# The end of the attention stage in a two-layer decoder trunk: when stored head outputs are read back, where one pair's output is kept, and which engine adds it up

## The chip, the core and the metric

One core of one Trainium2 chip runs the whole program in one launch. The metric is the device time of one execution in microseconds (us). The engines are TensorE (PE in the profile), VectorE (DVE), ScalarE (ACT), GpSimd (POOL) and SyncE (SP), which in this kernel issues nearly all DMAs.

## What is computed

A sequence of 1024 rows of width 1024 passes through two layers. Layer 0 is a recurrent mixer (RG-LRU) and a SwiGLU feed-forward network, layer 1 is stick-breaking attention with 16 heads of 64 columns and a second feed-forward network. Cut to the part that the change touches:

```python
def stick_breaking_attention(x, w_qkv, w_o):
    qkv = jnp.einsum("bsd,de->bse", x, w_qkv).reshape(bsz, seq, 3, N_HEADS, HEAD_DIM)
    ...
    for blk in range(seq // Q_BLOCK):
        z = jnp.einsum("bhqd,bhkd->bhqk", qb, kb).astype(jnp.float32) * scale
        strict = s_idx < t_idx
        log_fail = jnp.where(strict, jax.nn.log_sigmoid(-z), 0.0)
        suffix = lax.cumsum(log_fail, axis=3, reverse=True) - log_fail
        weights = jnp.where(strict, jnp.exp(jax.nn.log_sigmoid(z) + suffix), 0.0)
        outs.append(jnp.einsum("bhqk,bhkd->bhqd", weights.astype(vb.dtype), vb))
    o = jnp.concatenate(outs, axis=2)
    o = jnp.transpose(o, (0, 2, 1, 3)).reshape(bsz, seq, N_HEADS * HEAD_DIM)
    return jnp.einsum("bse,ed->bsd", o, w_o)
```

All is float32. The kernel splits each float32 operand of a dense product into a high and a low part and multiplies three times (`mm3`: high by high, high by low, low by high; lines 143, 144 and 145).

## The kernel before

**Pairs and halves.** The 16 heads are worked as 8 pairs, q = 0 to 7, and the sequence as two halves, n (or G) = 0 and 1, of 512 columns. The normalized input of the attention stands in SBUF as `xh[k][n]` and `xl[k][n]`, the high and low parts of row block k (128 rows of the model's width) and half n. The profile shows these buffers under the names of the tiles that had the space last: vh and vl, or xg. For each pair `qkv_steps` multiplies all eight row blocks with the pair's query, key and value weights (which = 0, 1, 2), 16 `mm3` each. The last reader of `xh` and `xl` is the value product of the last pair, (q, which) = (7, 2): first its eight row blocks for n = 0, then for n = 1.

**The loop.** The order of the work is written out by hand. A loop over u runs from -10 to 191; each u has one unit of `av_part` (a block of weights times values), one chunk of scores, two steps of the `qkv_steps` generator while it lasts, and a turn of small queued tasks. A chunk goes: PE makes scores (`z_part`, L1680 and L1681), ACT takes a sigmoid out of PSUM (`z_rest`, L1693), DVE scans it (`scan`, L1700 and L1703), ACT and DVE cut it into two 16-bit parts (`turn_weights`, L1713 and L1714, tile wx with four buffers), and SP issues a transposing DMA (L1717 to tile wd, L1721 to tile wt); other blocks are turned by PE itself (L1732) and cut by ACT (L1741) and DVE (L1742). PE then multiplies with the values (L1760). `last_two` is 168, the first unit of the last pair.

**Queued tasks.** `stage(task, steps)` holds a task for that many turns; `due()` runs what is due at the start of each u. `later` holds tasks of which each u runs one. The list `back` holds DMAs that read stored outputs back; each u issues one of them on SP (L1883), and from u = 160 on each even u two.

**Outputs.** A pair's output half (q, G) is gathered from PSUM by ACT (L1772) and DVE (L1773) into the tile oo, `add_v` adds a value term (tile vt) to it (L1777: GpSimd for the pairs 0 to 5, DVE for 6 and 7), and `parts` cuts it into a high part on ACT (L1784) and a low part on DVE (L1785). The output belongs into `xh[q]` and `xl[q]`, in which the normalized input still stands. So, for pairs that `kept(q, n)` names (0 to 5, and 6 for n = 0), `store` writes both parts to DRAM (tiles odh and odl, L1794 and L1795), and `bring_back` queues the reading back: for each half, once the last pair's value product of that half has been taken out of PSUM (L1610 to L1612).

**The values.** `evacuate` takes the value product out of PSUM (L1608), forms differences (L1613), and two turns later ACT makes a 16-bit copy (`high`, L1628), a turn later DVE its low part (L1618), and SP issues two transposing DMAs (L1622).

**What comes after.** From u = 163 on `out_fill` runs the first products of the output projection beside the last pair (tile ob, `mm3` with `xh[k][n]` for k = 0 to 6): one `mm3` in each of u = 163 to 168 for k = 0 to 5 of half 0, then k = 6 and the seven of half 1 in u = 177 to 180, then seven more from u = 182 on. The rest of the projection (tile ob_ps) and the second feed-forward network follow.

Of the kernel before, what the change touches and what calls it, by code (L numbers as in the profile page):

```python
# [34 lines left out]
def trunk(  # L35
# [21 lines left out]
    nc = tc.nc  # L57
# [84 lines left out]
    def mm3(ps, wh, wl, mh, ml, first, last, **kw):  # L142
        nc.tensor.matmul(ps, lhsT=wh, rhs=mh, start=first, stop=False, **kw)  # L143
        nc.tensor.matmul(ps, lhsT=wh, rhs=ml, start=False, stop=False, **kw)  # L144
        nc.tensor.matmul(ps, lhsT=wl, rhs=mh, start=False, stop=last, **kw)  # L145
# [1326 lines left out]
    NP = HEADS // 2  # L1472
# [3 lines left out]

    UP = 2.0**15

    kept = lambda q, n: q < NP - 2 + (n == 0)
    od = {  # L1480
        (q, n): [dp.tile([P, NB], F32, name=f"od{x}{q}_{n}") for x in "hl"]
        for n in range(NH)
# [5 lines left out]
    with ExitStack() as st:  # L1488
# [31 lines left out]
        def stage(task, steps=1):  # L1520
            soon.append([steps, task])
# [49 lines left out]
        def qkv_steps(q):  # L1571
            for which in range(3):
                w, at = wq.pop((q, which)), 3 * q + which + 1
                if at < 3 * NP:
                    raw = raws.pop(at)
                    wq[divmod(at, 3)] = next_weights(raw)
                    if which == 1:
                        later.extend(column_norms(raw, q))
                else:
                    mix[0].w[mix[0].order[0]] = next_weights(mix[0].raw.pop(0))  # L1580
                for i in (at + 1,) if at < 3 * NP else (at + 1, at + 2):
                    load_link(i)

                ks = (1, 5, 2, 6, 3, 7, 0, 4) if (q, which) == (0, 0) else range(ND)
                for n in range(NH):
                    pool, tag = (psZ, "z") if (q, which) == (0, 0) else (psQ, "qk")
                    ps = pool.tile([P, NB], F32, tag=tag, name="qk_ps")
                    for i, k in enumerate(ks):
                        mm3(ps, w[0][:, k], w[1][:, k], xh[k][n], xl[k][n], i == 0, i == ND - 1)
                        if i < ND - 1:  # L1590
                            yield
                    ev = evacuate(q, which, n, ps)
                    next(ev)
                    yield
                    next(ev, None)


        def evacuate(q, which, n, ps):
            full = lambda tag, m: [ap.tile([P, m, S], F32R, tag=tag, name=tag, bufs=4 if m == 1 else 3) for _ in range(2)]
            cs = slice(n * NB, (n + 1) * NB)  # L1600
            if which == 2:
                if n == 0:
                    VT[q] = ap.tile([P, S + 1], F32, tag="vt", name="vt", bufs=2)
                    nc.gpsimd.memset(VT[q][:, 0:1], 0.0)
                    VV[q] = ap.tile([P, 2, NT, 2, HD], F16, tag="v", name="v", bufs=2)
                t = ap.tile([P, NB], F32, tag="t", name="t", bufs=1)
                after = VT[q][:, n * NB + 1 : (n + 1) * NB + 1]
                nc.vector.scalar_tensor_tensor(after, ps, f32(sv[q]), rbc[n], op0=ALU.mult, op1=ALU.mult)  # L1608
                yield
                if q == NP - 1:  # L1610
                    some = [(p, n) for p in range(NP - 2)]
                    bring_back(*some[:3], *([(NP - 2, 0)] * n), *some[3:])  # L1612
                nc.vector.tensor_sub(t, VT[q][:, cs], after)  # L1613
                vx = ap.tile([P, 4, 2, P], F16, tag="vx", name="vx", bufs=2)
                t3 = t.rearrange("p (b c) -> p b c", b=4)

                def low():
                    nc.vector.scalar_tensor_tensor(  # L1618
                        vx[:, :, 1], t3, 1 / UP, vx[:, :, 0], op0=ALU.mult, op1=ALU.subtract
                    )  # L1620
                    for hx, a in enumerate((top, bot)):
                        nc.sync.dma_start(  # L1622
                            VV[q][:, hx, 4 * n : 4 * n + 4].rearrange("p b h c -> p (b h) c"),
                            vx[a].rearrange("p b h c -> p (b h c)"),
                            transpose=True,
                        )
                def high():
                    nc.scalar.activation(vx[:, :, 0], t3, AF.Copy, scale=1 / UP)  # L1628
                    stage(low)

                stage(high, 2)
                return
            two = ap.tile([P, 2, NB], F32R, tag="two", name="two", bufs=2)

            def spread():
                for hx, (a, b) in enumerate(((top, bot), (bot, top))):
                    if which == 0:
                        nc.sync.dma_start(f32(Q[q][hx])[a, cs], f32(two)[a, 0])
                        nc.sync.dma_start(f32(Q[q][hx])[b, cs], f32(two)[a, 1])
                    else:  # L1640
                        for half_ in (top, bot):
                            nc.sync.dma_start(f32(KK[q][hx])[half_, :, cs], f32(two)[a])

            def low():
                nc.vector.tensor_sub(two[:, 1], t, f32(two)[:, 0])
                stage(spread)

            if which == 0:
                t = ps
                if n == 0:  # L1650
                    Q[q] = [x[:, 0] for x in full("q", 1)]
                nc.scalar.copy(two[:, 0], t)
                yield
                low()
            else:
                t = f32(two)[:, 1]
                nc.vector.tensor_mul(t, ps, rbc[n])
                if n == 0:
                    KK[q] = full("kk", 2)
                yield  # L1660

                def high():
                    nc.scalar.copy(two[:, 0], t)
                    stage(low)

                stage(high)
# [80 lines left out]
        def av_part(tht, q, hx, G, kb, first, last):  # L1747
            q0 = (max(kb, 4 * G) - 4 * G) * P
            if first:
                av[0] = psO.tile([P, NB], F32, tag="o", name="av_ps")  # L1750
            ps = av[0]
            if kb // 4 != G:
                turned = [T[q, hx][:, 2 * kb + x].rearrange("p j c -> p (j c)") for x in range(2)]
                parts_ = [(0, NB, t, 0) for t in turned]
            else:
                parts_ = [(NB - P, NB, T[q, hx, 4 * G + 3][:, 2 * (kb % 4) + x], 0) for x in range(2)]
                if tht is not None:
                    parts_ = [(q0, NB - P, t, q0) for t in tht] + parts_
            for i, (c0, c1, t, t0) in enumerate(parts_):
                nc.tensor.matmul(  # L1760
                    ps[:, c0:c1], lhsT=VV[q][:, hx, kb], rhs=t[:, t0 : t0 + c1 - c0],
                    start=first and i == 0, stop=last and i == len(parts_) - 1,
                )
            if not last:
                return
            a, b = (top, bot)[:: 1 if hx == 0 else -1]

            def gather():
                if hx == 0:
                    oo[q, G] = ap.tile([P, NB], F32, tag="oo", name="oo", bufs=2)  # L1770
                o = oo[q, G]
                nc.scalar.copy(o[a], ps[b])  # L1772
                nc.vector.tensor_add(o[a], ps[a], o[a])  # L1773

            def add_v():
                eng = nc.vector if q >= NP - 2 else nc.gpsimd
                eng.tensor_add(oo[q, G], oo[q, G], VT[q][:, G * NB + 1 : (G + 1) * NB + 1])  # L1777

            def parts():
                o = oo[q, G]  # L1780
                down = f32(av_[q])

                def both(hi, lo):
                    nc.scalar.activation(hi, o, AF.Copy, scale=down)  # L1784
                    nc.vector.scalar_tensor_tensor(lo, o, down, f32(hi), op0=ALU.mult, op1=ALU.subtract)  # L1785

                if not kept(q, G):
                    both(xh[q][G], xl[q][G])
                else:
                    oh = ap.tile([P, NB], F32R, tag="oh", name="oh", bufs=1)  # L1790
                    both(oh, o.bitcast(F32R))

                    def store():
                        nc.sync.dma_start(od[q, G][0], f32(oh))  # L1794
                        nc.sync.dma_start(od[q, G][1], o)  # L1795

                    stage(store)

            later.insert(0, gather)
            if hx == 1:  # L1800
                later.extend((add_v, lambda: None, parts))
# [166 lines left out]
```

## Time and profile before

| what | value |
|---|---|
| runs of the kernel | 2139.91, 2144.06 and 2144.3 us, median 2144.06 us |
| the profiled execution's own time | 2142.03 us |
| its span, first to last instruction | 2140.0 us |
| PE, busy share of the span | 99% |
| DVE, busy share of the span | 83% |
| ACT, busy share of the span | 53% |
| POOL, busy share of the span | 6% |
| mean granted clock of TensorE | 0.997 |

The profiled execution's time is its span and 2.03 us around it. In the timelines a row gives the start, the length, the engine, the line of the kernel, the operation, output and inputs, and in brackets how long the engine was idle ahead of it and what ended that. In the lists of waits a row gives the engine and line that waited, what for, the total, the count and the longest. In the tables by stage a row gives each engine's busy time, the granted clock of TensorE as a share of full speed, the busy share of the 16 DMA engines and what they moved. The attention stage with its loop lies between about 980 and 1420 us of the span.

### The profile page before, as it was taken

To read this page: it belongs to the slowest core of one execution; us is meant where nothing else is said; L and a number is where in the kernel's file an instruction comes from. 1 tells how busy PE (TensorE), PEld (TensorE's weight loads), DVE (VectorE), ACT (ScalarE), POOL (GpSimd) and SP (SyncE) were. 2 spreads that over 40 slices of the span, in tenths; PEclk is the share of its full clock that TensorE was granted. 3 is DMA by queue.
4 is the path that set the end of the run, shared out by engine and by line. 5 is a ranking of instruction groups with operands and counts; after the bars stand their busy time and mean duration, and the time that the engine had idled before them with its cause. 6 is when DMAs were issued, how large, how long until landed. Compare 5 with 4: busy or idle time off the path is not lost.

```text
span 2140.0 us, 28244 instructions
## 1 busy us (share of the span) xinstructions
PE 2116.5 (99%) x10222; PEld 1735.1 (81%) x10222; DVE 1778.7 (83%) x2609; ACT 1137.5 (53%) x1838; POOL 125.8 (6%) x100
## 2 busy tenths in 40 slices
PE   8999999999999999999999999899999999999998
PEld 7888888888888888888777777678888888888887
DVE  7887768888888888896899999867888888888886
ACT  6567435444443545565666666544544344454556
POOL 1222020000000000000000000002000000000002
PEclk9999999999999999999999999999999999999999
DMA  7111421334445875536888888983234544587442
GB/s 237 50 50 40 153 98 58 117 113 157 138 148 162 276 241 148 160 121 143 160 177 178 176 177 177 230 257 99 64 104 128 162 135 151 193 274 229 130 153 89
DMA packets 424109, 323.87 MB, mean 151 GB/s; under 512 B 135065, under 2 KB 330785, under 8 KB 423969
## 3 DMA queue, kind: packets, MB, share of 16 engines
q1 hardware_dynamic: 423808, 321.80, 53.1%
q8 instruction: 80, 1.31, 0.3%
q14 instruction: 61, 0.49, 0.1%
q10 hardware_dynamic: 160, 0.27, 0.0%
HBM read 184.09 MB, written 83.36 MB: 125 GB/s over the span
## 4 chain that ended last, share of the span: by engine, by line
PE 96%; DVE 2%; DMA 1%; ACT 1%; issue 1%; SPq 0%; DVEq 0%; ACTq 0%
PE p_ps L143 18%; PE p_ps L145 18%; PE p_ps L144 18%; PE qk_ps L143 4%; PE qk_ps L145 4%; PE qk_ps L144 4%; PE av_ps L1760 3%; PE a_ps L144 3%; PE a_ps L145 3%; PE a_ps L143 3%; PE ob_ps L145 3%; PE ob_ps L143 3%; PE ob_ps L144 3%; PE z_ps L1680 2%; PE z_ps L1681 2%; PE i_ps L145 1%
## 5 line engine op out<-in xcount | busy, mean ns | idle before, releaser
L143 PE MATMUL p_ps<-vh,wbh 128*128 128x512 f32 x524 | 204.9, 391 | 0.0
L144 PE MATMUL p_ps<-vl,wbh 128*128 128x512 f32 x524 | 204.5, 390 | 0.0
L145 PE MATMUL p_ps<-vh,wbl 128*128 128x512 f32 x524 | 204.0, 389 | 0.2 <-DVE wbl L726 0.2
L143 PE MATMUL p_ps<-vh,wch 128*128 128x512 f32 x524 | 204.1, 390 | 0.0
L145 PE MATMUL p_ps<-vh,wcl 128*128 128x512 f32 x524 | 204.1, 389 | 0.0
L144 PE MATMUL p_ps<-vl,wch 128*128 128x512 f32 x524 | 203.9, 389 | 0.0
L722 ACT CAST wbh<-sb 128x1024 fp32r<-128x1024 f32 (+2 forms) x69 | 69.6, 1009 | 192.6 <-DVE sb L702 192.6
L1693 ACT ACTIVATE w<-z_ps,rs 128x128 f32<-128x128 f32 (+1 forms) x192 | 110.9, 580 | 94.0 <-PE z_ps L1681 93.5
L145 PE MATMUL p_ps<-vh,wal 128*128 128x512 f32 x396 | 154.0, 389 | 0.0
L143 PE MATMUL p_ps<-vh,wah 128*128 128x512 f32 x396 | 154.0, 389 | 0.0
L144 PE MATMUL p_ps<-vl,wah 128*128 128x512 f32 x396 | 154.0, 389 | 0.0
L145 PEld LDWEIGHTS p_ps<-vh,wbl 128*128 128x128 f32 x524 | 98.4, 188 | 21.6 <-DVE wbl L726 0.7
L145 PEld LDWEIGHTS p_ps<-vh,wcl 128*128 128x128 f32 x524 | 98.3, 188 | 21.0 <-DVE wcl L736 0.6
L144 PEld LDWEIGHTS p_ps<-vl,wch 128*128 128x128 f32 x524 | 98.4, 188 | 20.4
L143 PEld LDWEIGHTS p_ps<-vh,wch 128*128 128x128 f32 x524 | 98.3, 188 | 20.5 <-ACT tb L1181 0.2
L1700 DVE TENSOR_TENSOR_SCAN w<-w,unit 128x128 f32<-128x128 f32 (+3 forms) x128 | 105.0, 831 | 11.7 <-ACT w L1693 11.6
L143 PEld LDWEIGHTS p_ps<-vh,wbh 128*128 128x128 f32 x524 | 98.6, 188 | 19.8 <-ACT U L1181 0.4
L144 PEld LDWEIGHTS p_ps<-vl,wbh 128*128 128x128 f32 x524 | 98.6, 188 | 18.5
L143 PE MATMUL qk_ps<-vh,whi 128*128 128x512 f32 x264 | 111.9, 424 | 0.0
L145 PE MATMUL qk_ps<-vh,wlo 128*128 128x512 f32 x264 | 103.7, 393 | 0.0
L144 PE MATMUL qk_ps<-vl,whi 128*128 128x512 f32 x264 | 103.2, 391 | 0.0
L143 PE MATMUL p_ps<-vh,wd 128*128 128x512 f32 x254 | 99.4, 391 | 0.0
(403 smaller groups left out, 5794.2 us busy)
## 6 DMA issues: line engine op xcount, KB each, us to landing
raw<-in_ffn_w_in SPq DMA_DIRECT2D x88, 512.0 KB, 4.2
vl<-pd SPq DMA_DIRECT2D x128, 256.0 KB, 3.5
pd<-U SPq DMA_DIRECT2D x90, 256.0 KB, 2.3
kk<-two SPq DMA_DIRECT2D x64, 256.0 KB, 4.5
raw<-in_ffn_w_out SPq DMA_DIRECT2D x56, 256.0 KB, 3.7
raw<-in_attn_w_qkv SPq DMA_DIRECT2D x24, 512.0 KB, 5.9
h<-hd SPq DMA_DIRECT2D x32, 256.0 KB, 5.8
hd<-h SPq DMA_DIRECT2D x32, 256.0 KB, 2.0
```

Of the source, the lines that this page charges most:

```text
L143: nc.tensor.matmul(ps, lhsT=wh, rhs=mh, start=first, stop=False, **kw)
L144: nc.tensor.matmul(ps, lhsT=wh, rhs=ml, start=False, stop=False, **kw)
L145: nc.tensor.matmul(ps, lhsT=wl, rhs=mh, start=False, stop=last, **kw)
L722: nc.scalar.copy(self.full(self.wb), self.full(self.sb))
L1680: nc.tensor.matmul(ps[:, 0 : c1 - c0], lhsT=lhsT, rhs=KK[q][hx][:, 0, c0:c1], start=True, stop=False)
L1681: nc.tensor.matmul(ps[:, 0 : c1 - c0], lhsT=lhsT, rhs=KK[q][hx][:, 1, c0:c1], start=False, stop=True)
L1693: nc.scalar.activation(F, ps[:, 0:n], AF.Sigmoid, scale=rs[:, j : j + 1])
L1700: nc.vector.tensor_tensor_scan(rev, rev, unit[:, NB - n :][:, ::-1], 0.0, op0=ALU.mult, op1=ALU.add)
L1760: nc.tensor.matmul(ps[:, c0:c1], lhsT=VV[q][:, hx, kb], rhs=t[:, t0 : t0 + c1 - c0], start=first and i == 0, stop=last and i == len(parts_ ...
```

## The change

Four edits, all at the end of the attention stage:

- `kept` no longer names (6, 0). That output is not stored and read back; `parts` writes it straight into `xh[6][0]` and `xl[6][0]`.
- The reading back of (k, n), k = 0 to 5, is no longer queued for a whole half behind the value product's end. It is queued for each row block, two turns after the `mm3` of the last pair's value product that read this block last.
- `add_v` of pair 6 goes from DVE to GpSimd; pair 7 stays on DVE.
- The 16-bit copy of the last values, (7, 1), is made three turns after its product instead of two.

```diff
-    kept = lambda q, n: q < NP - 2 + (n == 0)
+    kept = lambda q, n: q < NP - 2
...
                     for i, k in enumerate(ks):
                         mm3(ps, w[0][:, k], w[1][:, k], xh[k][n], xl[k][n], i == 0, i == ND - 1)
+                        if (q, which) == (NP - 1, 2) and kept(k, n):
+                            stage(lambda k=k, n=n: bring_back((k, n)), 2)
                         if i < ND - 1:
                             yield
...
                 yield
-                if q == NP - 1:
-                    some = [(p, n) for p in range(NP - 2)]
-                    bring_back(*some[:3], *([(NP - 2, 0)] * n), *some[3:])
                 nc.vector.tensor_sub(t, VT[q][:, cs], after)
...
-                stage(high, 2)
+                stage(high, 3 if (q, n) == (NP - 1, 1) else 2)
...
             def add_v():
-                eng = nc.vector if q >= NP - 2 else nc.gpsimd
+                eng = nc.vector if q == NP - 1 else nc.gpsimd
                 eng.tensor_add(oo[q, G], oo[q, G], VT[q][:, G * NB + 1 : (G + 1) * NB + 1])
```

PE's instructions stand in the same order before and after. On SP the order changes as follows. The rows are from the last pair's stage; odh and odl with two numbers are the stored high and low parts of pair and half, wd and wt are transposed weights, kk is the last pair's key tile, v its value tile. Before:

```order
L1717 DMA_TRANSPOSE wd_12401<-wx_12398 128x8x128
L1721 DMA_TRANSPOSE wt_12435<-wx_12432 128x8x128
L1642 DMA kk_12272<-two_12351 64x2x512 x2
L1642 DMA kk_12273<-two_12351 64x2x512 x2
L1721 DMA_TRANSPOSE wt_12435<-wx_12468 128x8x128
L1721 DMA_TRANSPOSE wt_12435<-wx_12493 128x8x128
L1883 DMA vh0_3_2532<-odh0_0_7885 128x512
L1721 DMA_TRANSPOSE wt_12435<-wx_12537 128x8x128
L1883 DMA vl0_3_2533<-odl0_0_7886 128x512
L1622 DMA_TRANSPOSE v_12484<-vx_12500 128x8x64 x2
L1883 DMA xg0_6477<-odh1_0_7887 128x512
L1883 DMA xg1_6478<-odl1_0_7888 128x512
```

The same place on SP after the change:

```order
L1716 DMA_TRANSPOSE wd_12399<-wx_12396 128x8x128
L1882 DMA vh0_3_2532<-odh0_0_7885 128x512
L1720 DMA_TRANSPOSE wt_12434<-wx_12431 128x8x128
L1641 DMA kk_12270<-two_12349 64x2x512 x2
L1641 DMA kk_12271<-two_12349 64x2x512 x2
L1882 DMA vl0_3_2533<-odl0_0_7886 128x512
L1720 DMA_TRANSPOSE wt_12434<-wx_12468 128x8x128
L1882 DMA xg0_6477<-odh1_0_7887 128x512
L1720 DMA_TRANSPOSE wt_12434<-wx_12494 128x8x128
L1882 DMA xg1_6478<-odl1_0_7888 128x512
L1720 DMA_TRANSPOSE wt_12434<-wx_12538 128x8x128
L1882 DMA vh4_3_2540<-odh2_0_7889 128x512
```

Four returns now stand ahead of the last of the four wt transposes where one stood, the first of them ahead of the key spread. A little later on SP, before:

```order
L1883 DMA xg9_7656<-odl3_0_7892 128x512
L1622 DMA_TRANSPOSE v_12484<-vx_12606 128x8x64 x2
L1794 DMA odh6_0_7897<-oh_12642 128x512
L1795 DMA odl6_0_7898<-oo_12261 128x512
L1883 DMA vh2_3_2536<-odh4_0_7893 128x512
L1883 DMA vl2_3_2537<-odl4_0_7894 128x512
L1717 DMA_TRANSPOSE wd_12678<-wx_12675 128x8x128
L1883 DMA xg4_6481<-odh5_0_7895 128x512
```

And after the change:

```order
L1882 DMA xg9_7656<-odl3_0_7892 128x512
L1882 DMA vh2_3_2536<-odh4_0_7893 128x512
L1882 DMA vl2_3_2537<-odl4_0_7894 128x512
L1716 DMA_TRANSPOSE wd_12632<-wx_12629 128x8x128
L1882 DMA xg4_6481<-odh5_0_7895 128x512
L1882 DMA xg5_6482<-odl5_0_7896 128x512
L1882 DMA vh1_3_2534<-odh0_1_7897 128x512
L1716 DMA_TRANSPOSE wd_12673<-wx_12670 128x8x128
L1621 DMA_TRANSPOSE v_12484<-vx_12607 128x8x64 x2
```

The two stores are gone, and the second wd transpose stands ahead of the last values' two transposes instead of behind them and the stores. On DVE, where the first of the two adds of pair 6 stood, before:

```order
L1773 TENSOR_TENSOR oo_12261<-av_ps_12457,oo_12261 64x512
L1608 SCALAR_TENSOR_TENSOR vt_12482<-qk_ps_12501,sv_12415,rbc1_84 128x512
L1700 SCALAR_TENSOR_TENSOR w_12601<-w_12601,unit_7926 128x512
L1777 TENSOR_TENSOR oo_12261<-oo_12261,vt_11853 128x512
L1613 TENSOR_TENSOR t_12595<-vt_12482 128x512
```

The same place on DVE after the change:

```order
L1772 TENSOR_TENSOR oo_12259<-av_ps_12457,oo_12259 64x512
L1610 SCALAR_TENSOR_TENSOR vt_12482<-qk_ps_12502,sv_12413,rbc1_84 128x512
L1699 SCALAR_TENSOR_TENSOR w_12602<-w_12602,unit_7924 128x512
L1612 TENSOR_TENSOR t_12596<-vt_12482 128x512
L1699 SCALAR_TENSOR_TENSOR w4_12611<-w4_12611,unit_7924 128x128
```

The add of L1777 is missing there, and also further down, where the second add of pair 6 stood; POOL has both in their place.

## The prediction

> **What bounds the kernel now.** I read the page first, then PE's waits over the whole span, then the table by stage around the longest of them, and last the timelines of SP, PE and DVE there.
>
> ```profile
> PE 2116.5 (99%) x10222; PEld 1735.1 (81%) x10222; DVE 1778.7 (83%) x2609; ACT 1137.5 (53%) x1838; POOL 125.8 (6%) x100
> ```
>
> PE is busy 99% of the span, so a change elsewhere can only win what PE loses. That is 2140.0 - 2116.5 = 23.5 us, and the largest part of it that has a name is one place:
>
> ```profile
> PE ob L143 <- DMA vh<-odh: 4.2, 3, 1.7
> ...
> PE z_ps L1680 <- ACT w L1693: 2.5, 3, 1.9
> PE ob L144 <- DMA vl<-odl: 1.4, 3, 1.0
> PE ob L144 <- DMA xg<-odl: 1.1, 1, 1.1
> ```
>
> Three of these rows are the first projection products (ob) waiting for returned outputs: 4.2 + 1.4 + 1.1 = 6.7 us. They lie between 1367 and 1389. The table by stage shows what goes on around them:
>
> ```profile
> core 0: us, PE busy (x) PEld busy (x) DVE busy (x) ACT busy (x) POOL busy (x), PEclk, DMA share, GB/s
> 1300.00:1366.00 66.00, 66.00 (x368) 50.38 (x367) 61.86 (x96) 44.13 (x86) 6.65 (x8) 1.00 0.90 179
> 1366.00:1411.00 45.00, 34.65 (x166) 22.31 (x166) 39.23 (x56) 25.75 (x50) 2.89 (x2) 0.89 1.05 260
> 1411.00:1430.00 19.00, 19.00 (x100) 14.64 (x100) 11.03 (x16) 8.19 (x13) 0.00 (x0) 1.00 0.97 305
> ```
>
> Ahead of 1366 and behind 1411 PE has no gap. In the 45 us between, it is busy 34.65, part of it at a lower granted clock (0.89 in the mean). The reader is to see DVE beside it: 39.23 of 45. So PE has over 10 us of slack in this stage, and DVE has only 45 - 39.23 = 5.8. The stage ends at 1411 when the last scans and cuts are done, not when the returns are. **What the change can win is bounded by DVE, not by the 6.7 us of PE's waits.**
>
> **Part by part: the returns.** SP issues everything in order, and its queue is full here:
>
> ```profile
> 1352.55 2.31 SPq L1717 DMA_TRANSPOSE wd<-wx  x1
> 1356.32 2.21 SPq L1721 DMA_TRANSPOSE wt<-wx  x1
> 1358.59 3.40 SPq L1642 DMA_DIRECT2D kk<-two  x4
> 1362.08 4.48 SPq L1721 DMA_TRANSPOSE wt<-wx  x2
> 1366.66 0.58 SPq L1883 DMA_DIRECT2D vh<-odh  x1
> 1367.33 1.26 SPq L1721 DMA_TRANSPOSE wt<-wx  x1
> 1368.64 0.57 SPq L1883 DMA_DIRECT2D vl<-odl  x1
> 1369.32 2.51 SPq L1622 DMA_TRANSPOSE v<-vx  x2
> ...
> 1373.45 0.42 SPq L1883 DMA_DIRECT2D vl<-odl  x1
> ...
> 1379.81 0.53 SPq L1794 DMA_DIRECT2D odh<-oh  x1
> 1380.39 0.42 SPq L1795 DMA_DIRECT2D odl<-oo  x1
> ...
> 1382.08 1.24 SPq L1717 DMA_TRANSPOSE wd<-wx  x1
> ```
>
> And PE where the returns are used:
>
> ```profile
> 1367.81 0.34 PE L1681 MATMUL z_ps<-kk,q 128*128 128x384 f32 x1
> 1369.89 0.80 PE L143 MATMUL ob<-vh,whi 128*128 128x512 f32 x1 [1.74 <-DMA vh<-odh]
> 1371.64 0.79 PE L144 MATMUL ob<-vl,whi 128*128 128x512 f32 x1 [0.96 <-DMA vl<-odl]
> ...
> 1374.72 1.08 PE L1760 MATMUL av_ps<-wt,v 128*128 128x512 f16 x2
> ...
> 1379.01 0.50 PE L144 MATMUL ob<-vl,whi 128*128 128x512 f32 x1 [0.20 <-DMA vl<-odl]
> ```
>
> After the change the first return stands ahead of the wt of 1356.32. SP is idle from 1354.86 to 1356.32, so it costs the queue nothing and lands before 1360. The second stands right behind the key spread, at 1362.0, and lands by about 1366 (3.2 us from 1366.66 to 1369.89 for the first one now). PE needs them at about 1368, so the first wait goes, and so do those from the fourth block on, whose returns are issued some 6 us earlier. What is late next on PE is the last wt transpose. Now it is issued at 1367.33, and PE, held up, uses it at 1374.72. After the change three returns of about 0.5 stand ahead of it and one of 0.58 no longer does: about 1368.3. PE without its wait would be there at about 1370. So part of the first wait comes back as a wait for wt until 1372. The whole of the 6.7 us does not return on PE either.
>
> **The second wd transpose.** ACT and DVE lose time to it:
>
> ```profile
> ACT wx L1713 <- DMA wd<-wx: 2.9, 1, 2.9
> ...
> DVE wx L1714 <- ACT wx L1713: 2.7, 3, 1.5
> DVE w L1700 <- ACT w L1693: 1.3, 2, 0.8
> DVE w L1703 <- ACT w L1693: 0.9, 1, 0.9
> ```
>
> The wd of 1382.08 was ready when DVE had cut it, at 1377.1, and stood 5 us behind the last values' pair, the two stores and two returns. ACT waited 2.9 for its buffer, and DVE 1.5 for ACT. After the change it stands ahead of the values' pair, and the stores are gone. The values' transposes go later by this one issue (1.24), which nobody in these rows waits for. DVE's other waits, 1.3 + 0.9, are for sigmoids of scores that PE made late. So DVE's idle time is what the change works on: of 5.8 us these rows name 4.9.
>
> **The adds of pair 6 go to POOL.** DVE loses two instructions of 0.67, 1.3 in all:
>
> ```profile
> L1777 DVE TENSOR_TENSOR oo<-oo,vt 128x512 f32<-128x512 f32 x2 | 1.3, 666 | 0.0
> 1314.32 1.10 POOL L1777 TENSOR_TENSOR oo<-oo,vt 128x512 f32<-128x512 f32 x1 [12.13 <-DVE oo L1773]
> 1314.93 1.56 DVE L1700 TENSOR_TENSOR_SCAN w<-w,unit 128x512 f32<-128x512 f32 x1
> 1332.22 2.13 POOL L1777 TENSOR_TENSOR oo<-oo,vt 128x512 f32<-128x512 f32 x1 [16.81 <-DVE oo L1773]
> 1333.38 1.52 DVE L1714 TENSOR_TENSOR wx<-w,wx 128x512 f16<-128x512 f32 x1
> 1363.33 0.67 DVE L1714 TENSOR_TENSOR wx<-w,wx 128x512 f16<-128x512 f32 x1
> 1368.59 1.21 DVE L1700 TENSOR_TENSOR_SCAN w<-w,unit 128x512 f32<-128x512 f32 x1
> ```
>
> But it does not win 1.3. The rows of pair 5 show what an add on POOL does to DVE: the scan beside the first takes 1.56 instead of 1.21 (+0.35), the cut beside the second 1.52 instead of 0.67 (+0.85). In pair 6 the first add has the same neighbours on DVE (gather, value product, a 512-wide scan). For the second I take the 0.85 of the nearest row. The bounds are 0 (nothing beside it) and 1.1 (the add's own length) each. Net: -1.3 + 0.35 + 0.85 = -0.1 us on DVE, between -1.3 and +0.9. ACT's cut behind the add waits up to 1.46 longer (2.13 - 0.67); it stands two turns, some 4 us, later, which hides that.
>
> The Trainium skill, "SBUF — State Buffer", section "SBUF: two separate sides", says that DVE (with two SBUF inputs) and GpSimd lock each other out of a shared port pair for a whole instruction. Taken literally each add would stop DVE for 1.10, and the sum below would be (39.23 - 1.33 + 2.2) / 0.937 = 42.8, a gain of 2.2 instead of 3.3. The traced lengthening is smaller, since DVE meets only part of the add, and I go by the rows.
>
> **Written in place, and the later copy.** The write into block 6 of half 0 must wait until the value product has read it; that read stands at u = 156, the write no earlier than u = 161, so it does not wait. It takes two stores and two returns of about 0.5 each from SP and as many transfers from the DMA engines, which are busy here (share 1.05). The later copy moves ACT's L1628 behind two sigmoids; it had waited 0.6 for DVE there. I price both at 0 beside the terms above: SP is not waited for except in the ways named.
>
> **The sum.** DVE's work in the stage becomes 39.23 - 0.1 = 39.1. How tightly can it run? In the undisturbed stage ahead, with PE never waiting, it was busy 61.86 of 66, 93.7%. At that share 39.1 us of work take 41.7, so the stage shrinks by **3.3 us**. The bounds: 5.9 if DVE never idles, 0 if it idles as now. The rest of the kernel is PE without gaps, so the end moves by the same. From the profiled execution's 2142.03 that gives 2138.7. This execution lies 2.0 below the median of the runs, and the mean of all four times is 2142.6, which gives 2139.3. I forecast **2139.0 us**, 0.24% below the median shown. About 0.2%, 4.3 us, is what a measurement of this kernel can tell from no change, so 2139.8 is the border.
>
> **The rivals.**
>
> *SP's order sets the pace instead of DVE.* Behind the last wt stand a return, two value transposes (2.51) and the low half of block 2, whose landing at 1379.0 released PE above. By the sums above it is issued at 1368.3 + 1.3 + 0.6 + 2.5 = 1372.7 instead of 1373.45, so PE starts block 2 only 0.8 earlier. If all behind follows that: 2142.6 - 0.8 = 2141.8. For it: SP is full in these rows. Against it: DVE did not wait for PE until 1374.5, and the later returns and the wd go earlier by more. Chance 0.17.
>
> *Slower.* The same transposes come so late that PE gets them later than now. It decides when the last wt lands after 1374.7. With the worst rows, three returns of 1.13 (the longest of L1883) and a transpose of 3.13 (the longest of L1721) and 5.5 to landing:
>
> ```profile
> L1883 SPq DMA_DIRECT2D vh<-odh x8: 314/456/1127, 1366.7 to 1398.6; - x8
> ...
> L1721 SPq DMA_TRANSPOSE wt<-wx x13: 1231/1261/3131, 1339.5 to 1410.7; - x13
> ...
> DMA to landing us min/median/max: 3.1/3.8/5.5
> ```
>
> 1367.33 + 3.4 - 0.6 + 1.9 + 5.5 = 1377.5, that is 2.8 later than 1374.7: 2145.4. The last pair's own four wt transposes also have returns between them; hit alike, they make it 2148.2, and 2148.4 is the border on this side. Against it: the median landing, 3.8, gives 1372. Chance 0.10, of which 0.06 beyond the border.
>
> *DVE closes all its gaps:* 2142.6 - 5.9 = 2136.7. For it: 4.9 of its 5.8 us idle have causes that the change removes. Against it: at 1300 to 1366 it never ran above 94%. Chance 0.15.
>
> *No effect:* PE's waits for returns only become waits for sigmoids, and 1411 stays: 2142.6. Chance 0.03.
>
> **How the numbers follow.** The forecast has 0.55, of which 0.37 lies below the border and 0.18 above. Faster: 0.37 + 0.15 = 0.52. Same: 0.18 + 0.17 + 0.03 + 0.04 = 0.42. Slower: 0.06. The range reaches from the lowest run less 5.9, 2139.91 - 5.9 = 2134.0, to 2144.5, which leaves out the worse part of the slower rival.
>
> **What would show it.** Right: PE's rows on odh and odl gone or under 2 us, and new waits of ob, z_ps or av_ps for wt, L1693 or L1742; DVE's share of the stage near 94%; ACT's 2.9 for wd gone; two DVE rows lengthened beside POOL's adds. Wrong: DVE below 90% with PE still waiting for DMAs (then SP sets the pace), or the stage shorter than 39.1 us, which would break the bound on DVE.

## The result, and the profile after

| kernel | median of its runs, us | lowest to highest | ratio to before, 95% interval |
|---|---|---|---|
| before (22 runs) | 2143.17 | 2139.91 to 2147.7 | |
| after (22 runs) | 2138.84 | 2137.36 to 2140.86 | 0.9981, 0.9975 to 0.9987 |

The forecast was 2139.0. The change wins 4.3 us, 0.2% of the time, and the interval lies below 1. The profiled execution of after took 2138.37 us with a span of 2136.4, against 2142.03 and 2140.0 before. In after the numbers of the lines from the scores on are one lower than in before (L1679 and L1680 are the scores, L1692 the sigmoid, L1699 and L1702 the scans, L1712 and L1713 the cuts, L1716 and L1720 the transposes wd and wt, L1882 the returns).

The page's row of engines, and then the rows of PE's waits over the whole span that lie in the stage, in after:

```profile
PE 2117.5 (99%) x10222; PEld 1737.7 (81%) x10222; DVE 1776.7 (83%) x2607; ACT 1136.9 (53%) x1838; POOL 131.8 (6%) x102
```

```profile
PE z_ps L1679 <- ACT w L1692: 6.0, 5, 1.9
...
PE av_ps L1759 <- DVE tl L1741: 1.3, 3, 0.8
```

All rows in which PE waits for a returned output (odh, odl; 6.7 us before) are gone. In a second traced execution of after one is left:

```profile
1375.82 0.50 PE L144 MATMUL ob<-vl,whi 128*128 128x512 f32 x1 [1.92 <-DMA vl<-odl]
```

The row of scores that wait for a sigmoid has grown from 2.5 to 6.0 us. The row of the stage itself in the table by stage (the columns are those of the prediction's table):

```profile
1366.30:1408.10 41.80, 34.39 (x169) 22.91 (x169) 38.48 (x54) 25.16 (x50) 5.80 (x4) 0.88 1.11 250
```

The first projection product behind the stage begins at 1408.38, where before it began at 1411.56. The stage has shrunk from 45 to 41.8 us; DVE is busy 38.48 of them, 92%.

What set the time is plainest in the chain of waits (start, length, what; a DMA's length runs from its issue to its landing). Three stretches of before:

```profile
1373.45 5.52 DMA vl<-odl
1379.01 0.50 PE ob L144
...
1384.53 0.94 SPq L1721
1385.47 0.04 issue
1385.51 3.26 DMA xg<-odl
1388.82 0.49 PE ob L144
```

And the same time in after:

```profile
1381.30 0.33 DVE tl L1741
...
1382.12 1.26 DVE wx L1713 x2
1383.38 1.20 DVE w L1702
1384.58 0.33 DVE w L1699
1384.91 0.12 issue
1385.03 0.63 ACT wx L1712
1385.68 0.57 DVE wx L1713
```

Before, the chain runs through SP's queue and two returned low parts; DVE is busy beside it, but does not carry it. In after no DMA stands in the chain between 1366 and 1408: it goes from DVE to ACT and back. Some of its pieces (2.13 and 2.97 us of "issue" ahead of L1712) name no releaser. Ahead of the second of them a DVE scan ends at 1406.08 and ACT's cut begins at 1406.15, so DVE is the likely one there too.

### The profile page after: what moved, and what is told of

It reads as the page before. It is cut to its first block, busy times and chain, and to the rows that moved or that the text cites. A ratio compares the mean times of both kernels' runs of the same rounds, so it can differ in the third digit from the quotient of the medians.

```text
span 2136.4 us, 28240 instructions
## 1 busy us (share of the span) xinstructions
PE 2117.5 (99%) x10222; PEld 1737.7 (81%) x10222; DVE 1776.7 (83%) x2607; ACT 1136.9 (53%) x1838; POOL 131.8 (6%) x102
## 4 chain that ended last, share of the span: by engine, by line
PE 96%; DVE 2%; ACT 1%; issue 1%; DMA 0%; SPq 0%; DVEq 0%; ACTq 0%
PE p_ps L143 18%; PE p_ps L145 18%; PE p_ps L144 18%; PE qk_ps L143 4%; PE qk_ps L145 4%; PE qk_ps L144 4%; PE av_ps L1759 3%; PE a_ps L144 3%; PE a_ps L145 3%; PE a_ps L143 3%; PE ob_ps L143 3%; PE ob_ps L145 3%; PE ob_ps L144 3%; PE z_ps L1679 2%; PE z_ps L1680 1%; PE i_ps L145 1%
## 5 line engine op out<-in xcount | busy, mean ns | idle before, releaser
L1692 ACT ACTIVATE w<-z_ps,rs 128x128 f32<-128x128 f32 (+1 forms) x192 | 110.9, 580 | 90.8 <-PE z_ps L1680 88.8
L1699 DVE TENSOR_TENSOR_SCAN w<-w,unit 128x128 f32<-128x128 f32 (+3 forms) x128 | 105.3, 833 | 10.5 <-ACT w L1692 10.4
```

Of the source, the lines that this page charges most:

```text
L1692: nc.scalar.activation(F, ps[:, 0:n], AF.Sigmoid, scale=rs[:, j : j + 1])
L1699: nc.vector.tensor_tensor_scan(rev, rev, unit[:, NB - n :][:, ::-1], 0.0, op0=ALU.mult, op1=ALU.add)
```

## The experiments

Each median below the first two rows is that of 11 runs, beside runs of before on the same chip. "Against after" takes the 2138.5 of the second run of after, or its first 2138.8, which differ by less than can be told: the intervals leave each ratio of 11 runs open by 0.0009 to either side, that is 1.9 us. Differences under 2 us are therefore not shown by the medians alone.

| kernel | median, us | before beside it | ratio to before, 95% interval | against after, us | stage in its trace, us | DVE busy in it, us |
|---|---|---|---|---|---|---|
| before (the runs above) | 2143.17 | | | | 45.7 | 39.9 (87%) |
| after (the runs above) | 2138.84 | 2143.17 | 0.9981, 0.9975 to 0.9987 | | 42.3 | 38.8 (92%) |
| returns per row block alone | 2142.11 | 2142.65 | 0.9997, 0.9988 to 1.0006 | +3.3 | 44.4 | 39.7 (89%) |
| written in place alone | 2141.10 | 2142.65 | 0.9993, 0.9984 to 1.0002 | +2.3 | 44.3 | 39.9 (90%) |
| adds on GpSimd alone | 2142.53 | 2142.65 | 0.9999, 0.9990 to 1.0008 | +3.7 | 44.1 | 38.9 (88%) |
| returns and in place | 2140.87 | 2142.55 | 0.9993, 0.9984 to 1.0002 | +2.0 to 2.3 | 43.1 | 39.7 (92%) |
| the same and the later copy (after without the adds) | 2140.01 | 2142.65 | 0.9985, 0.9976 to 0.9994 | +1.2 to 1.5 | 43.0 | 39.7 (92%) |
| after, second time | 2138.54 | 2143.06 | 0.9982, 0.9973 to 0.9991 | | 42.1 | 38.8 (92%) |
| after, DVE +6 cuts | 2143.55 | 2143.06 | 1.0002, 0.9993 to 1.0011 | +5.0 | 46.6 | 43.0 (92%) |
| after, 6 cuts from DVE to ACT | 2139.53 | 2143.06 | 0.9983, 0.9974 to 0.9992 | +1.0 | 42.2 | 35.4 (84%) |
| after, 6 cuts off DVE | 2138.62 | 2142.55 | 0.9981, 0.9973 to 0.9990 | 0 | 41.0 | 35.3 (86%) |
| after, SP +6 copies of 256 KB | 2142.17 | 2143.06 | 0.9995, 0.9986 to 1.0004 | +3.6 | 44.6 | 38.9 (87%) |
| after, SP +6 copies of 2 KB | 2142.12 | 2142.62 | 0.9997, 0.9988 to 1.0006 | +3.6 | 45.1 | 38.9 (86%) |
| after, returns issued by GpSimd | 2144.24 | 2142.55 | 1.0011, 1.0002 to 1.0020 | +5.7 | 47.0 | 39.1 (83%) |

The last two columns are from the one traced execution of each kernel: the stage from the start of the same score product on PE to the start of the first product of the projection behind it (1365.83 to 1411.56 in before, 1366.12 to 1408.38 in after), and DVE's work in it. They leave out what varies in the rest of the kernel, but each is a single execution: the two of after differ by 0.1, and PE's granted clock in the stage lies anywhere between 0.85 and 0.96. The traced executions of before and after differ by 3.7 us, 3.5 of them in the stage. Where medians and stages disagree, the price of a part is not shown.

For the second run of after:

> The kernel after itself, once more, as the base for the three runs beside it. From its 22 runs: a median within 0.7 us of 2138.8, if the kernel before is again within 0.7 us of 2142.9.

It came out as expected, and is the base for what follows. Two theories stood against each other. **A:** DVE's work sets the pace of the stage; the change wins because it takes away what made DVE idle. **B:** SP's order, with the transposes that stand in it, sets the pace; the change wins because it empties and reorders that queue.

### The parts of the change

**Returns per row block alone**, on before:

```diff
                         mm3(ps, w[0][:, k], w[1][:, k], xh[k][n], xl[k][n], i == 0, i == ND - 1)
+                        if (q, which) == (NP - 1, 2) and k < NP - 2:
+                            stage(lambda some=((k, n), (NP - 2, 0))[: 1 + ((k, n) == (2, 1))]: bring_back(*some), 2)
...
-                if q == NP - 1:
-                    some = [(p, n) for p in range(NP - 2)]
-                    bring_back(*some[:3], *([(NP - 2, 0)] * n), *some[3:])
```

> Before, with only the returns of the blocks 0 to 5 queued per row block. The output (6,0) is still stored and read back (its return is queued behind the third block of half 1), pair 6 stays on DVE, the last copy stays at two turns. Theory A (DVE sets the pace of the stage, and the early returns take away what made it idle): PE's rows for odh and odl fall below 1 us except perhaps one for block 6, and most of the 4.3 us difference of the two medians is here: 2 to 4.5 us below the kernel before, near 2140. Rival B (SP's load counts: the two stores and two returns of (6,0), 2 to 2.5 us on SP in the same stretch, are what had to go): under 1.5 us below the kernel before, with PE still waiting for a DMA.

It won 0.5 us (1.3 in the traced stage). Theory A expected most of the 4.3 us here. That was not so, though PE's waits for returns did shrink, to one of 1.4. ACT's waits for DMAs in this kernel's stage show where it went:

```profile
ACT wx L1712 <- DMA wd<-wx: 4.1, 1, 4.1
```

The wait for the second wd transpose has not gone but grown, from 2.9 to 4.1.

**Written in place alone**, on before:

```diff
-    kept = lambda q, n: q < NP - 2 + (n == 0)
+    kept = lambda q, n: q < NP - 2
...
-                    some = [(p, n) for p in range(NP - 2)]
-                    bring_back(*some[:3], *([(NP - 2, 0)] * n), *some[3:])
+                    bring_back(*[(p, n) for p in range(NP - 2)])
```

> Before, with only the output (6,0) written in place; the returns of the other blocks stay queued for a whole half, the add and the copy as before. Theory A: PE's 4.2 us for the first returns stay as they are, and so does nearly all of the time: 0 to 1 us below the kernel before. Rival B (SP's load counts): two stores and two returns less let the second wd transpose and the values' pair go some 2 us earlier, ACT's 2.9 us for wd shrink, and 1.5 to 3 us are won.

It won 1.6 us (1.4 in the traced stage), in rival B's range, and ACT no longer waited for wd by name. Its interval holds 1, so the size is not certain.

**Adds on GpSimd alone**, on before:

```diff
-                eng = nc.vector if q >= NP - 2 else nc.gpsimd
+                eng = nc.vector if q == NP - 1 else nc.gpsimd
```

> Before, with only the two adds of pair 6 on GpSimd. The prediction's price: 1.3 us less on DVE, 0.35 and 0.85 us more by instructions that are lengthened beside the adds, so 0 within 0.5 us. Rival C (the adds win what they take off DVE, because the second one lengthens nothing): 0.9 to 1.3 us below the kernel before. Rival D (each add stops DVE for its whole length): 0.9 us above.

By the medians 0.1 us, but the interval reaches some 2 us to either side and holds the prediction's price and both rivals. It does take 1.0 us of work off DVE (the second add fell into a stretch where DVE was idle). The traced stage is 1.6 us shorter than the one of before, but PE's granted clock was 0.96 in it and 0.89 in that of before. Whether the adds win anything as long as returns and wd are late stays open.

**After without the adds on GpSimd** (the same line the other way round):

> The kernel after, with the two adds of pair 6 back on DVE. Where DVE is what sets the pace, 1.33 us of work come back and the 0.35 us that the first add lengthened a scan by go: 0.5 to 1.3 us above the kernel after. By the prediction's net of -0.1 us it would be 0 to 0.3 above. If SP or PE sets the pace: 0, within 0.5.

1.2 us above the first runs of after and 1.5 above the second, and 0.7 to 0.9 in the traced stages, with 0.8 us more work on DVE at the same 92%. Both point to DVE's work counting once the returns are out of the way; the run with more work on DVE, below, shows it clearly. That the same edit is worth less on before, as 0.1 beside 1.2 to 1.5 suggests, is not shown.

**Returns and in place together**, with the copy at two turns and the adds on DVE:

```diff
-                stage(high, 3 if (q, n) == (NP - 1, 1) else 2)
+                stage(high, 2)
...
-                eng = nc.vector if q == NP - 1 else nc.gpsimd
+                eng = nc.vector if q >= NP - 2 else nc.gpsimd
```

> Before, with the returns per row block and (6,0) written in place, and nothing else (pair 6 on DVE, the last copy at two turns). Alone the first gave -0.5 us and the second -1.5 us against the kernel before. If they add up: 2.0 below it, near 2141. If they need each other (the returns moved forward stand ahead of the second wd transpose, and only the missing stores and returns let it go early): 2.5 to 4 below, near 2139.5, with no wait of ACT for wd. Beside the run with the later copy too (2140.0), it also prices that copy: the prediction has 0.

1.7 us below before: the two add up (0.5 and 1.6), within what is measured, and so do the traced stages (1.3 and 1.4 alone, 2.7 together). DVE is busy 92% of the stage here, as in after; in before and with one part alone it is 87 to 90%. So with these two parts DVE takes over the pace. ACT still waits 2.8 for wd here, and the kernel with the later copy too lies 0.9 us lower. SP's queue tells what the copy changes. In the kernel with both parts and the early copy:

```profile
1374.42 1.24 SPq L1716 DMA_TRANSPOSE wd<-wx  x1
...
1376.38 2.68 SPq L1621 DMA_TRANSPOSE v<-vx  x2
1379.11 0.58 SPq L1882 DMA_DIRECT2D xg<-odl  x1
1379.73 0.44 SPq L1882 DMA_DIRECT2D vh<-odh  x1
1380.29 1.24 SPq L1716 DMA_TRANSPOSE wd<-wx  x1
```

In the kernel that also has the later copy:

```profile
1374.08 1.24 SPq L1716 DMA_TRANSPOSE wd<-wx  x1
...
1377.23 1.93 SPq L1716 DMA_TRANSPOSE wd<-wx  x1
1379.26 2.52 SPq L1621 DMA_TRANSPOSE v<-vx  x2
```

Copying the last values a turn later moves their two transposes from ahead of the second wd to behind it, and wd goes 3 us earlier (2.3, as the stage began 0.8 earlier in that execution). That order is the work of this edit, and of no other. What it wins is not shown. ACT's cut that needs wd stands in the two kernels at

```profile
1384.88 0.62 ACT L1712 CAST wx<-w 128x512 f16<-128x512 f32 x1 [2.78 <-DMA wd<-wx]
```

```profile
1384.03 0.62 ACT L1712 CAST wx<-w 128x512 f16<-128x512 f32 x1 [2.10 <-DVE w L1699]
```

Counted from the start of the stage that is 19.2 us with the early copy and 19.1 with the later one: without the wait for wd, DVE's scan lets ACT begin no earlier. The steps of the ladder, 1.7, 0.9 and 1.2 to 1.5 us (2.7, 0.1 and 0.7 in the traced stages), are each less than the medians can tell; their sum is sure.

### What sets the pace of after

**DVE more:**

```diff
             nc.vector.tensor_sub(wx[:, :, 1], F, wx[:, :, 0])
+            if (q, hx) == (NP - 1, 0):
+                nc.vector.tensor_sub(wx[:, :, 1], F, wx[:, :, 0])
```

> The kernel after, with the low part of the turned weights of head (7,0) subtracted twice over, with the same result: six more instructions of 0.67 us alone or 0.60 in a run of them, 3.6 to 4.0 us more DVE work between 1366 and 1400. Theory A (DVE at 92% sets the pace of the stage): 2.5 to 4.3 us above the kernel after (4.0 / 0.92 at most), with PE's and ACT's waits for DVE grown. Rival B (SP's transfers, or the path from score to weight, set the pace and DVE only happens to be busy): under 1 us.

5.0 us above after: theory A, and more than the 4.3 that it allowed. The traced stage is 4.3 longer, with DVE at 92% of it as in after, and the 0.7 between the two is less than the medians can tell.

**SP more:**

```diff
+        again = [dp.tile([P, NB], F32, name=f"again{k}") for k in range(NP - 2)]
...
+                    if n == 0 and x == 0:
+                        back[-1] += (again[q],)
...
-                        nc.sync.dma_start(*back.pop(0))
+                        dst, src, *more = back.pop(0)
+                        nc.sync.dma_start(dst, src)
+                        for m in more:
+                            nc.sync.dma_start(m, src)
```

> The kernel after, with a copy of 256 KB from DRAM to DRAM issued on SP behind each of the six returns of high parts of half 0: six more issues of some 0.5 us, 3 us more on SP between 1355 and 1378, and 1.5 MB more for the DMA engines. Theory A with a slack SP: the returns and transposes come 0.5 to 3 us later, PE shows waits for odl, wt or wd again, and the time rises by at most 1.5 us, since DVE still has the most work. Rival B (SP and the DMA engines set the pace): 2 to 4 us above the kernel after.

3.6 us above after (2.3 in the traced stage): that is rival B's range. And with hardly any bytes in the same places:

```diff
-        again = [dp.tile([P, NB], F32, name=f"again{k}") for k in range(NP - 2)]
+        again = [dp.tile([P, 4], F32, name=f"again{k}") for k in range(NP - 2)]
...
-                            nc.sync.dma_start(m, src)
+                            nc.sync.dma_start(m, src[:, 0:4])
```

> The kernel after, with the six extra copies of the run that cost 3.6 us, but of 16 bytes a row instead of 2 KB: the same six places on SP (some 0.5 us each, 3 us in all), next to no bytes. If it was the place on SP that cost the time (the transposes behind it are issued 3 us later): again 2.5 to 4 us above the kernel after. If it was the 1.5 MB on the DMA engines (6 us at the 250 GB/s that this stage moves): under 1 us above it.

3.6 again (2.8 in the traced stage). It is the place on SP that costs, not the 1.5 MB; the DMA engines' busy share of the stage is 1.02 here, against 1.11 in after. In the timeline of SP of the kernel with the small copies the two wd transposes come at

```profile
1378.82 1.26 SPq L1719 DMA_TRANSPOSE wd<-wx  x1
...
1382.99 1.25 SPq L1719 DMA_TRANSPOSE wd<-wx  x1
```

instead of 1375.10 and 1378.23 (the stage itself began 0.8 later here), and its chain and ACT's waits show them in front:

```profile
1376.49 5.81 DMA xg<-odl
...
1382.99 5.24 DMA wd<-wx
...
1388.62 0.63 ACT wx L1715
```

```profile
ACT wx L1715 <- DMA wd<-wx: 4.9, 2, 2.9
```

So both theories' additions cost about their full size. Work is only shown to be the limit, though, if taking it away also wins.

**DVE less, ACT more:**

```diff
-            nc.vector.tensor_sub(wx[:, :, 1], F, wx[:, :, 0])
+            if (q, hx) == (NP - 1, 0):
+                nc.scalar.copy(wx[:, :, 1], F)
+            else:
+                nc.vector.tensor_sub(wx[:, :, 1], F, wx[:, :, 0])
```

> The kernel after, with six of DVE's subtractions (the low part of the turned weights of head (7,0)) left out: ACT writes a second 16-bit copy of the weights there, six more instructions of 0.62 us on ACT, so this part of the attention is computed from doubled weights. DVE's work falls by 3.6 to 4.0 us, ACT's rises by 3.7 on some 25 of 42. Theory A: the stage shrinks again, 1.5 to 4 us below the kernel after; the floor is where PE, then at 34.4 us of work part of it at half clock, has no gap left. Rival B: within 1 us of the kernel after.

1.0 us above after instead of 1.5 to 4 below, and the traced stage is as long as that of after. ACT's copies may have eaten the gain, so once more without them:

```diff
+            if (q, hx) == (NP - 1, 0):
+                nc.gpsimd.memset(wx[:, :, 1], 0.0)
+            else:
+                nc.vector.tensor_sub(wx[:, :, 1], F, wx[:, :, 0])
```

> The kernel after, with the same six subtractions of head (7,0) taken off DVE as in the run that gave ACT a copy for each, but here GpSimd writes zeros instead, ahead of the data, so the low parts of those weights are missing from the products; ACT's work is that of the kernel after. If DVE's work sets the pace and it was ACT's six copies that ate the gain: 1.5 to 4 us below the kernel after. If SP's order and the path through ACT set it, and DVE is only as busy as they let it: within 0.7 us of it, and ACT's waits for the wd transpose appear as in the other run.

Within 0.2 us of after. The traced stage is 1.2 us shorter, which the medians cannot tell; wd took 5.3 us to land in it, where it took 6.4 in after. The groups of DVE between 1366 and 1411 (count, then busy us and mean ns, then idle ahead and its cause), first the cuts in after, then two groups of this kernel:

```profile
L1713 DVE TENSOR_TENSOR wx<-w,wx 128x512 f16<-128x512 f32 x12 | 8.1, 680 | 2.7 <-ACT wx L1712 2.6
```

```profile
L1744 DVE TENSOR_TENSOR tl<-wt_ps,th 128x128 f16<-128x128 f32 (+2 forms) x13 | 5.0, 409 | 5.4 <-ACT th L1743 5.3
L1716 DVE TENSOR_TENSOR wx<-w,wx 128x512 f16<-128x512 f32 x6 | 4.1, 681 | 1.3 <-ACT wx L1712 1.2
```

DVE has 4.0 us less to do and waits 5.3 for ACT ahead of the low parts tl, where it waited 1.2 in after. ACT's queue was held by the wd transpose; here is this kernel's chain:

```profile
1370.90 1.20 SPq L1621
...
1376.10 1.24 SPq L1719
...
1379.38 5.33 DMA wd<-wx
1384.81 0.62 ACT wx L1712
```

And the time to landing of the second wd in after, issued there at 1378.23:

```profile
DMA to landing us min/median/max: 6.4/6.4/6.4
```

1378.23 + 6.4 = 1384.6. ACT's cut started at 1385.03, when DVE's scans let it. **The two paths end within half a microsecond of each other.** Neither theory was right by itself: DVE carries the chain in after, and SP's path stands right behind. Lengthen either, and the time grows by about as much; shorten DVE's alone, and the other one holds. No run here shortens both.

**The returns off SP:**

```diff
-                        nc.sync.dma_start(*back.pop(0))
+                        nc.gpsimd.dma_start(*back.pop(0))
```

> The kernel after, with the 24 returns issued by GpSimd instead of SP: 24 issues of 0.4 to 1.1 us, 13 us in all, leave SP between 1354 and 1397, and the transposes of weights and values go as soon as their data is there. If SP's order sets the pace beside DVE: 1 to 3 us below the kernel after. If DVE alone does: within 0.7. No trace here shows a DMA issued by GpSimd; if its issues take more than the 1.3 us that lie between two of them, the returns come late again and PE waits for odh and odl: 0 to 4 us above.

5.7 us above after, and above before (1.0011, 1.0002 to 1.0020). GpSimd's issues took 0.54 each, so the issues were not what was slow. In this kernel's timeline of GpSimd seven returns follow each other almost without a gap from 1356.7 to 1360.5, a time in which SP in after issues none, and SP's own queue stalls:

```profile
1358.58 3.10 SPq L1641 DMA_DIRECT2D kk<-two  x4
1361.77 10.61 SPq L1720 DMA_TRANSPOSE wt<-wx  x3
```

The key spread kk took 9.9 us to land, against 4.0 to 5.1 in after, and PE waited for it:

```profile
1369.74 0.36 PE L1679 MATMUL z_ps<-kk,q 128*128 128x256 f32 x1 [2.56 <-DMA kk<-two]
1377.28 1.01 PE L1759 MATMUL av_ps<-wt,v 128*128 128x512 f16 x2 [3.98 <-issue]
```

In after SP's own order spaces the returns between the transposes. That the crowd of returns is what held kk up follows from the rows' places alone; another queue with the same spacing was not tried. A rival stays open beside it: the profile books these returns on another queue (software_dynamic, 1920 packets) than SP's, and their median landing was 5.7 us, against 4.2 in after. The Trainium skill, "DMA: Bandwidth & Descriptors", section "Rules for kernel authors", says that spreading DMAs over several issuing engines does not help, since all use the same 16 DMA engines, and only saves issue time. It did not help here either: some 13 us of issues left SP, and the time rose by 5.7.

## Why the prediction was right, and where not

**The returns: right.** All of PE's waits for them went in the first traced execution and all but one of 1.9 us in the second, and the last wt transpose was issued at 1367.99 (forecast 1368.3). **The wait that takes their place: right in size by luck, wrong in its cause.** It was forecast for wt until 1372. It came as

```profile
1371.63 0.65 PE L1679 MATMUL z_ps<-kk,q 128*128 128x512 f32 x1 [1.91 <-ACT w L1692]
```

PE's order has a score ahead of the product with wt. ACT had its sigmoid behind a cut that waited for a DVE scan (such waits of ACT add up to 6.1 us in the stage), so DVE's lateness reached PE through ACT.

**"What the change can win is bounded by DVE, not by the 6.7 us": the number held, the reasoning fell short.** It read DVE's busy share. The chain of before shows that returned low parts carried the stage from 1373 to 1389, and DVE took over only once the returns and the place of (6,0) were both changed (92% of the stage from there on). DVE alone does not set what can be won: with 4.0 us less of work the time does not fall, since SP's path stands behind. The first rival, SP's order, was the right mechanism for before. Its price, 0.8 us, was wrong: it followed one return (block 2) and not what stands behind it on SP, the wd and the return of 1385.51 that the chain of before goes through.

**The second wd: right that it goes, wrong in what makes it go.** The prediction let it pass the values' pair without saying by which edit, and priced the later copy at 0. It is the later copy that does it, though ACT's wait for wd by name also went with the place of (6,0) alone. Its price of 0 is not refuted: the medians put 0.9 us on it, less than they can tell, and the traced stages 0.1.

**Written in place: priced at 0, measured 1.6 us** alone (1.4 in the traced stage), with an interval that holds 1. The words "SP is not waited for except in the ways named" are the step that failed: in after, some 3 us of SP in front of wd cost 3.6 us (2.8 in the traced stage), as the six small copies showed.

**The adds: mis-sized.** The first lengthened the scan beside it by just the 0.35 forecast; for the second 0.85 were taken and it was 0. GpSimd and DVE around the two adds in after:

```profile
1368.28 1.09 POOL L1776 TENSOR_TENSOR oo<-oo,vt 128x512 f32<-128x512 f32 x1 [12.14 <-DVE oo L1772]
1387.98 1.80 POOL L1776 TENSOR_TENSOR oo<-oo,vt 128x512 f32<-128x512 f32 x1 [18.61 <-PE z_ps L1680]
```

```profile
1368.89 1.56 DVE L1699 TENSOR_TENSOR_SCAN w<-w,unit 128x512 f32<-128x512 f32 x1
...
1387.93 0.96 DVE L1699 TENSOR_TENSOR_SCAN w<-w,unit 128x384 f32<-128x384 f32 x1
```

Net DVE saved 1.3 - 0.35 = 1.0 us, not 0.1. The Trainium skill's rule of the lock ("SBUF — State Buffer", "SBUF: two separate sides") fits better than the prediction read it, since the one that starts first keeps the ports. At 1368.28 the add is first, and the scan that starts at 1368.89 meets 0.48 us of it (and is 0.35 longer). At 1387.93 the scan is first, and it is the add that becomes 0.71 longer. Who starts first is the question, not the add's length.

**The sum: right, partly by two errors that cancel.** DVE's work was 38.48 us, not 39.1, and its share 92%, not 93.7%: 41.8 us against the forecast 41.7. At 93.7% the stage would have been 41.1. That the time, 2138.84, meets the 2139.0 so closely is luck in part: the sum took 3.3 us off a base of 2142.6, and the medians differ by 4.3 from a base of 2143.17. **The rivals:** the slower one did not come (PE has no wait for wt), but the runs with three more microseconds on SP show how near it stood: they give back 3.6 of the 4.3 us that the change wins.

## What to carry to other kernels

A busy share tells how much work an engine has, the chain of waits tells who carries the end; read the chain of the stage first, and ask of each path what it costs longer and what it wins shorter. An issuing engine's queue is a resource like the others: here six issues of half a microsecond in front of transposes that somebody waits for cost 3.6 us, whatever their bytes, and an edit that looks like a delay (a later copy) can let another issue pass. Two paths that end together hide each other: work put on either costs its full size, and work taken off one wins next to nothing. And where a step of the ladder is no larger than what the medians can tell, its price is open, however well a mechanism for it reads.

## What the runs showed of the hardware

After a gap of 1.9 us PE's matmuls ran at about half their pace for a while, with a granted clock of 0.55 between 1371.6 and 1375.4. In after's timeline of PE, with starts 0.23 apart ahead of the gap, some 0.43 apart behind it, and 0.23 again from 1375.40:

```profile
1369.20 0.40 PE L1680 MATMUL z_ps<-kk,q 128*128 128x512 f32 x1
1369.44 0.29 PE L1759 MATMUL av_ps<-wd,v 128*128 128x128 f16 x2
...
1373.81 0.63 PE L144 MATMUL ob<-xg,whi 128*128 128x512 f32 x1
1374.23 0.63 PE L145 MATMUL ob<-xg,wlo 128*128 128x512 f32 x1
1374.66 0.63 PE L1679 MATMUL z_ps<-kk,q 128*128 128x512 f32 x1
...
1375.40 0.39 PE L143 MATMUL ob<-vh,whi 128*128 128x512 f32 x1
1375.63 0.39 PE L144 MATMUL ob<-vl,whi 128*128 128x512 f32 x1
```

From 1371.63 to 1375.40 this costs PE as much again as the gap itself, some 1.9 us. A gap of 0.82 at 1389 had no such end. Nor had every gap of 1.9 us: in the second traced execution of after the same wait of 1.91 ends at 1371.16, and from 1372.59 on the starts are 0.23 apart again; the slow stretch comes there behind a second gap, of 1.92 at 1375.82, and lasts from about 1377 to 1380.6. The Trainium skill, "TensorE: Matmul & The Clock Gate", section "Part 1: The HAM clock gate", has the clock halved after an idle window of about 3.4 us; here it came behind gaps of 1.9 us, though not behind each of them.
